# The steps of each head's softmax placed one by one, with longer planned durations for ScalarE and VectorE from attention on

## The chip, the cores and the metric

The kernel runs on one core of a Trainium2 chip. The metric is the device time of one execution in microseconds; the number quoted for the kernel before is the median of its timed runs. Engines are named as in the profile: PE is the matrix engine (PEld its weight loads), ACT is ScalarE, DVE is VectorE, POOL is GpSimd, SP is the queue that starts most DMAs.

## The reference, cut to what matters

One layer of a hybrid block over 528 tokens (16 meta tokens and 512 others) and 2048 channels. One projection gives the inputs of two branches. Branch A is attention of 8 heads with 4 key groups, in which an indexer picks 128 keys for each query; branch B is a gated linear recurrence. Each branch is gated, multiplied by its own 1024x2048 matrix, weighted by a sigmoid gate and added; the sum goes through a 2048x2048 output matrix.

```python
logits = einsum('bqgrd,bqkgd->bqgrk', qg, k_sel) * scale
logits = where(valid, logits, -inf)
p = softmax(logits, axis=-1)
o = einsum('bqgrk,bqkgd->bqgrd', p, v_sel)          # branch A, 8 heads
y_a = o * silu(z_a)
...
p = einsum('btnc,ncd->btnd', y, w_branch)           # two branches, 1024 -> 2048
merged = sum(sigmoid(gates) * p, axis=2)
return x + merged @ w_out                           # 2048 -> 2048
```

## The kernel before, in words

Everything is kept in 32 bits; a product of full accuracy is made of three matmuls, high by high, low by high and high by low. So each weight chunk of 128x1024 is split on the chip: ACT rounds it into `wh` (L387), DVE subtracts into `wl` (L388). The chunks stream through six buffers `raw`, and three buffers each for `wh` and `wl`. The chunk that a job of PE multiplies was split during the job before it, so a new `wh` can be written only when PE has left the job that used that buffer.

The program runs in stages. First the input projection in jobs of one or two column blocks (`run_pair`, products `px`, `py`, `pz`, `pw`), with the indexer and the recurrence between them. Then 32 branch jobs, 16 for branch B and 16 for branch A: each is 8 blocks of 3 matmuls of 128x512 into one PSUM bank `pg` (`mm3`, 24 matmuls), after which DVE multiplies the bank by the gate (`d_br`, tile `mg`). Last the output projection (`run_out`, `po`). Attention has no stage of its own: it is laid between the 24 matmuls of the branch B jobs.

A head h of attention is two tasks. `att_task(h)` loads its queries (and for an even head its group's keys and values, `kv`) by POOL's queue, lets PE make the logits (`plg`, four query tiles of 528, 400, 272 and 144 keys, in 15 matmuls), lets DVE add the mask and take the row maximum (L898, into `lg`), negates the maxima (L903), lets ACT take four exponentials with row sums (L906), lets DVE take the reciprocals (L908) and lets ACT scale the four tiles (L911). `pv_task(h)` then turns the probabilities by PE transposes into `ppt`, copies them by ACT into `pT`, `pS` and `pTH` (DVE makes the low parts `pTL` and that of `pS`), multiplies them with the values into `pov`, and lets DVE multiply by the gate tile `za`, which a DMA of POOL's queue brings (L959).

The order of all engines is written by a planner when the program is built. `Core` keeps a clock for each engine; `at` (L56) adds a cost to it for each instruction recorded, and the cost of ACT is 60 ns and 0.833 ns for each element of a row, that of DVE's two-operand form 65 ns and 1.042 ns. A task is a generator: it records some instructions and yields the planned time from which it may go on. `pump` (L223) is called after each block of 3 matmuls: it steps every task whose time, with 300 ns added, lies before PE's clock, and records what the task has next. Each engine then works strictly in the order recorded, waiting on semaphores. A PSUM bank that a task gets may still have to be read by ACT or DVE from its last use; PE then waits.

Of the kernel before, what the change touches and what calls it, by code (L numbers as in the profile page):

```python
# [13 lines left out]
OP = mybir.AluOpType  # L14
# [16 lines left out]
WAIT = object()  # L31
# [14 lines left out]
class Core:  # L46
# [3 lines left out]
    def __init__(self, nc):  # L50
        self.nc = nc
        self.clk = {"pe": 0.0, "act": 0.0, "dve": 0.0, "pool": 0.0}
        self.wr = {}
        self.ac = {}

    def at(self, eng, cost, outs, ins):  # L56
        t = self.clk[eng]
        for a in ins:
            w = self.wr.get(a.tensor.name)
            if w:  # L60
                t = max(t, w[0] + (SAME[eng] if w[1] == eng else LAT))
        for a in outs:
            w = self.ac.get(a.tensor.name)
            if w:
                t = max(t, w[0] + (0 if w[1] == eng else LAT))
        e = t + cost
        self.clk[eng] = e
        for a in ins:
            w = self.ac.get(a.tensor.name)
            if not w or w[0] < e:  # L70
                self.ac[a.tensor.name] = (e, eng)
        for a in outs:
            self.wr[a.tensor.name] = (e, eng)
            self.ac[a.tensor.name] = (e, eng)
        return e + LAT
# [24 lines left out]
    def act(self, out, in_, f, **kw):  # L100
        self.nc.scalar.activation(out, in_, f, **kw)  # L101
        outs = [out] + ([kw["accum_out"]] if "accum_out" in kw else [])
        ins = [in_] + [v for v in kw.values() if not isinstance(v, (int, float)) and v is not kw.get("accum_out")]
        return self.at("act", 60 + 0.833 * self.n(in_), outs, ins)

    def tt(self, out, a, b, op):
        self.nc.vector.tensor_tensor(out, a, b, op=op)  # L107
# [75 lines left out]
def hybrid_kernel(ctx, tc, x, meta, vecs, w_in, rows, w_branch, w_out,  # L183
# [7 lines left out]
    E = Core(nc)  # L191
# [23 lines left out]
    def spawn(gen, prio=1):  # L215
        t = Task(gen, prio)
        i = len(tasks)
        while i and tasks[i - 1].prio > prio:
            i -= 1
        tasks.insert(i, t)  # L220
        return t
# [41 lines left out]
    def slot(name, dt=F32):  # L263
        return S.get(name, dt)
# [529 lines left out]
    def vs_task():  # L794
        while len(stored) < 17:
            yield WAIT
        yield from room(9)
        vx3.extend((slot("vS", F32R), slot("pS", F32R), slot("pS", F32R), slot("v3")))
        vS, v3 = vx3[0], vx3[3]
        nc.gpsimd.dma_start(v3[:, :512], v3d)  # L800
        vx = slot("vx")
        nc.gpsimd.dma_start(vx[:, :64], vxd)
        for t in vx3[:3]:
            E.pool([t], [], T // 2, lambda v: v.memset(t[:96, :512].bitcast(F32), 0.0))
        yield E.clk["pe"] + 6000.0
        pm = yield from bank("pvm")
        for g in range(4):
            e = E.tr(pm[:16, 128 * g:128 * g + 128], vx[:, 16 * g:16 * g + 16], ident)
        S.put(vx)
        yield e  # L810
        E.act(vS[0:16, :512], pm[:16], AF.Copy)
        E.act(vS[32:48, :512], pm[:16], AF.Copy)
        e = E.tt(vS[64:80, :512], pm[:16], vS[0:16, :512].bitcast(F32), OP.subtract)
        B1.put(pm)
        yield e
# [36 lines left out]
    att = {}  # L852

    def att_task(h):
        g = h // 2
        while not vx3 or h and att.get(h - 1, 0) < 1 or not topk_done():
            yield WAIT
        yield from room(2 if g in kTH else 6, 6)
        qH, qL = slot("qH", F32R), slot("qL", F32R)
        for i, t in enumerate((qH, qL)):  # L860
            nc.gpsimd.dma_start(t[:, :512].bitcast(F32), qd_[h][i])
        if g not in kTH:
            for d, src, n in ((kTH, kd_[g][0], T), (kTL, kd_[g][1], T), (vH, vd_[g][0], 512), (vL, vd_[g][1], 512)):
                d[g] = slot("kv", F32R)
                nc.gpsimd.dma_start(d[g][:, :n].bitcast(F32), src)
        yield E.clk["pe"] + 10000.0
        while h and att[h - 1] < 2 or len(S.free) < 8:
            yield WAIT
        sm = small[h % 2]
        ps, pbs, vs = {}, {}, {}  # L870
        for qt in (3, 2, 1, 0):
            kq = KQ[qt]
            sl = slice(128 * qt, 128 * qt + 128)
            if kq > 512:
                pb = yield from pair("plg")
                parts = [(pb[:, c, :264], slice(264 * c, 264 * c + 264)) for c in range(2)]
                vs[qt] = pb[:, :, :264]
            else:
                if qt:
                    pb = yield from bank("plg")  # L880
                vs[qt] = pb[:, :kq] if qt else pb[:, KQ[1]:KQ[1] + kq]
                parts = [(vs[qt], slice(0, kq))]
            pbs[qt] = pb
            for o, ks in parts:
                E.mm(o, qH[:, sl], kTH[g][:, ks], True, False)
                E.mm(o, qH[:, sl], kTL[g][:, ks], False, False)
                e = E.mm(o, qL[:, sl], kTH[g][:, ks], False, True)
            if qt == 3:
                e3 = e
        S.put(qH, qL)  # L890
        att[h] = 1
        yield e3 + 600
        col = lambda qt, i: sm[:, 4 * qt + i:4 * qt + i + 1]
        for qt in (3, 2, 1, 0):
            kq = KQ[qt]
            xs = ps[qt] = slot("lg")
            f2 = (lambda a: a.rearrange("p (a b) -> p a b", a=2)) if kq > 512 else (lambda a: a)
            E.dve([xs, sm], [pbs[qt], bias[qt]], kq, lambda vv: vv.tensor_tensor_reduce(  # L898
                f2(xs[:, :kq]), vs[qt], f2(bias[qt][:, :]), SC, NEG, OP.add, OP.max, col(qt, 0)))
            if qt != 1:  # L900
                (B2 if kq > 512 else B1).put(pbs[qt])
        allc = lambda i: sm.rearrange("p (q i) -> p q i", i=4)[:, :, i]
        E.ts(allc(1), allc(0), -1.0, None, OP.mult)  # L903
        for qt in (3, 2, 1, 0):
            xs = ps[qt][:, :KQ[qt]]
            e = E.act(xs, xs, AF.Exp, bias=col(qt, 1), accum_out=col(qt, 2))  # L906
        yield e + 1200
        E.dve([sm], [sm], 4, lambda vv: vv.reciprocal(allc(3), allc(2)))  # L908
        for qt in (3, 2, 1, 0):
            xs = ps[qt][:, :KQ[qt]]  # L910
            e = E.act(xs, xs, AF.Copy, scale=col(qt, 3))  # L911
        att[h] = 2
        pv_tasks.append(spawn(pv_task(h, ps, e + 1000), 1))

    pv_tasks = []

    def pv_task(h, ps, e):
        g = h // 2
# [21 lines left out]
        pb, e = yield from turn(3)  # L940
        yield e
        for b in (3, -1, 0, 1, 2):
            n = 512 - 128 * max(b, 0)
            kp = 128 if b >= 0 else 16
            if b == 3:
                tH, tL = slot("pT"), None
                e = E.act(tH[:, :n], pb[:, :n], AF.Copy)
            elif b < 0:
                E.act(pS[0:16, :n], pb[:16, :n], AF.Copy)
                E.act(pS[64:80, :n], pb[:16, :n], AF.Copy)  # L950
                e = E.tt(pS[32:48, :n], pb[:16, :n], pS[0:16, :n].bitcast(F32), OP.subtract)
            else:
                tH, tL = slot("pTH", F32R), slot("pTL", F32R)
                E.act(tH[:, :n], pb[:, :n], AF.Copy)
                e = E.tt(tL[:, :n], pb[:, :n], tH[:, :n].bitcast(F32), OP.subtract)
            B1.put(pb)
            if b == 3:
                z = slot("za")
                nc.gpsimd.dma_start(z[:, :512], zad[h])  # L959
            if b != 2:  # L960
                pb, e2 = yield from turn(0 if b == -1 else (-1 if b == 3 else b + 1))
            yield e
            o = po[:, 512 - n:]
            if b == 3:
                E.mm(o, v3[:, gs], tH[:, :n], True, False, loose=True)
                S.put(tH)
            elif b < 0:
                E.mm(o, vS[:96, gs], pS[:96, :n], False, False, loose=True)
            else:
                wh, wl = vH[g][:, 128 * b:128 * b + 128], vL[g][:, 128 * b:128 * b + 128]  # L970
                E.mm(o, wh, tH[:, :n], False, False, loose=True)
                E.mm(o, wh, tL[:, :n], False, False, loose=True)
                e = E.mm(o, wl, tH[:, :n], False, b == 2, loose=True)
                S.put(tH, tL)
        yield e
        e = E.tt(z[:, :512], po, z[:, :512], OP.mult)
# [593 lines left out]
    jobs = [Job("in", C_KI, 80, True, done=d_kiwi)]  # L1570
# [33 lines left out]
            gate_pair()  # L1604
    while gates:
        gate_pair()
    jobs[-1].pre = lambda: (spawn(vs_task(), 1), [spawn(att_task(h), 1) for h in range(8)])
    pairs = [j for j in jobs if j.kind == "pair"]
    for n in (1, 0):
        for p in range(8):  # L1610
# [213 lines left out]
```

## Time and profile before

| | us |
|---|---|
| timed runs: median of 3 (lowest, highest) | 1529.73 (1529.63, 1530.08) |
| the profiled execution's own time | 1525.58 |
| its span, first to last instruction | 1523.8 |
| DVE busy in the span | 1173.5 (77%) |
| ACT busy in the span | 679.5 (45%) |
| POOL busy in the span | 199.4 (13%) |

The profile is of one execution, which took 4.15 us less than the median of the timed runs; the two are kept apart below. In the span attention lies at about 1130 to 1260 us. Busy time of PE is the union of its matmul records; a record lasts longer than the distance from one matmul to the next (a 128x512 record some 0.40 us, the next one starting 0.23 us later), so the first 0.17 us of a pause do not show as idle.

### The profile page before, as it was taken

The page shows a single profiled execution, that of the slowest core. Times are in us where ns is not written, and L with a number is a line of the kernel's source. Part 1 is how long each engine was busy: PE and PEld are TensorE (multiplying, and loading weights), DVE is VectorE, ACT ScalarE, POOL GpSimd, SP SyncE. Part 2 cuts the span into 40 slices and gives each one's busy share as a digit, 9 for nine tenths or more (in the row PEclk, how much of TensorE's full clock was granted, in tenths as well). Part 3 has the DMA queues.
Part 4 walks back from the last instruction along what each step waited for, and adds up shares of the span by engine and source line. Part 5 has one row for each costly group of instructions (what it writes and reads, how often), then busy time and mean ns, then how long its engine had stood idle before and what let it go on. Part 6 is the DMA issues. An engine that isn't in the chain of part 4 may idle for free.

```text
span 1523.8 us, 30986 instructions
## 1 busy us (share of the span) xinstructions
PE 1500.0 (98%) x12648; PEld 1417.8 (93%) x12648; DVE 1173.5 (77%) x1971; ACT 679.5 (45%) x1048; POOL 199.4 (13%) x241
## 2 busy tenths in 40 slices
PE   7999999999999999999999999999999999999998
PEld 6888899999999999999999999999998778889998
DVE  7799999999998778677768776786665455878675
ACT  5555454444444443443443444444455652334332
POOL 3100000001111101001000010000032210102222
PEclk9999999999999999999999999999999999999999
DMA  9223368867787756766675667567796434448773
GB/s 267 83 70 83 96 158 190 186 162 187 200 205 198 194 134 142 180 149 161 146 174 133 160 157 177 143 142 174 188 296 216 160 118 125 143 139 216 212 212 89
DMA packets 300959, 250.08 MB, mean 164 GB/s; under 512 B 12932, under 2 KB 267920, under 8 KB 300816
## 3 DMA queue, kind: packets, MB, share of 16 engines
q1 hardware_dynamic: 274080, 167.95, 37.6%
q0 software_dynamic: 20656, 72.81, 24.2%
q10 hardware_dynamic: 6080, 7.34, 1.4%
q8 instruction: 99, 1.62, 0.4%
q14 instruction: 44, 0.36, 0.1%
HBM read 168.00 MB, written 27.62 MB: 128 GB/s over the span
## 4 chain that ended last, share of the span: by engine, by line
PE 86%; issue 7%; ACT 2%; DVE 2%; POOL 1%; DMA 1%; ACTq 0%; POOLq 0%; DVEq 0%
PE pg L93 18%; PE pz L91 14%; PE py L91 14%; PE px L91 14%; PE po L91 10%; PE pw L91 7%; PE phl L93 1%; PE psc L93 1%; ACT lg L101 1%; PE pho L93 1%; PE pov L91 1%; PE phs L93 1%; DVE lg L898 1%; PE px L97 1%; DMA kv<-vd 1%
## 5 line engine op out<-in xcount | busy, mean ns | idle before, releaser
L101 ACT ACTIVATE wh<-raw 128x1024 fp32r<-128x1024 f32 x304 | 322.0, 1060 | 490.1 <-PE pz L91 130.6
L107 DVE TENSOR_TENSOR wl<-raw,wh 128x1024 fp32r<-128x1024 f32 x302 | 370.9, 1229 | 140.7 <-ACT wh L101 139.0
L91 PE MATMUL px<-hH,wh 128*128 128x256 f32 (+1 forms) x672 | 193.5, 288 | 0.0
L91 PE MATMUL px<-hH,wl 128*128 128x256 f32 (+1 forms) x672 | 189.2, 282 | 0.0
L91 PE MATMUL px<-hL,wh 128*128 128x256 f32 (+1 forms) x672 | 189.2, 281 | 0.0
L101 ACT ACTIVATE wh<-sum 128x1024 fp32r<-128x1024 f32 x100 | 106.1, 1061 | 181.5 <-PE pw L91 70.7
L91 PE MATMUL po<-wh,mh 128*128 128x256 f32 x896 | 158.5, 280 | 0.5 <-DVE xq L107 0.5
L107 DVE TENSOR_TENSOR wl<-sum,wh 128x1024 fp32r<-128x1024 f32 x100 | 127.0, 1270 | 34.4 <-ACT wh L101 34.3
L91 PEld LDWEIGHTS po<-wh,mh 128*128 128x128 f32 x896 | 137.4, 189 | 0.8 <-DVE xq L107 0.7
L91 PEld LDWEIGHTS px<-hH,wh 128*128 128x128 f32 x672 | 126.5, 188 | 0.9
L91 PEld LDWEIGHTS px<-hH,wl 128*128 128x128 f32 x672 | 126.6, 188 | 0.0
L91 PEld LDWEIGHTS px<-hL,wh 128*128 128x128 f32 x672 | 126.4, 188 | 0.0
L91 PE MATMUL po<-wl,mh 128*128 128x256 f32 x448 | 125.6, 280 | 0.0
L91 PE MATMUL py<-tT,wh 128*128 128x256 f32 (+1 forms) x672 | 124.7, 284 | 0.0
L91 PE MATMUL pw<-tT,wh 128*128 128x256 f32 (+1 forms) x672 | 124.6, 285 | 0.0
L91 PE MATMUL pz<-tT,wh 128*128 128x256 f32 (+1 forms) x672 | 123.5, 283 | 0.0
L116 POOL DMA_DIRECT2D raw<-raw x50 | 43.2, 863 | 519.9 <-DVE sum L107 510.1
L91 PEld LDWEIGHTS py<-tT,wh 128*128 128x128 f32 x672 | 103.3, 188 | 0.5
L91 PEld LDWEIGHTS pw<-tT,wh 128*128 128x128 f32 x672 | 103.2, 188 | 0.2
L91 PEld LDWEIGHTS pz<-tT,wh 128*128 128x128 f32 x672 | 103.1, 188 | 0.2
L93 PE MATMUL pg<-yH,wh 128*128 128x512 f32 x256 | 103.0, 402 | 0.1
L93 PE MATMUL pg<-yL,wh 128*128 128x512 f32 x256 | 100.8, 394 | 0.0
(317 smaller groups left out, 3792.8 us busy)
## 6 DMA issues: line engine op xcount, KB each, us to landing
raw<-in_w_in_dram SPq DMA_DIRECT2D x192, 512.0 KB, 4.6
raw<-raw POOLq DMA_DIRECT2D x50, 512.0 KB, 5.3
raw<-sum POOLq DMA_DIRECT2D x50, 512.0 KB, 6.1
raw<-in_w_branch_dram SPq DMA_DIRECT2D x32, 512.0 KB, 5.0
raw<-in_w_out_dram SPq DMA_DIRECT2D x32, 512.0 KB, 4.3
gd<-g SPq DMA_DIRECT2D x32, 256.0 KB, 5.1
g<-gd POOLq DMA_DIRECT2D x30, 256.0 KB, 3.4
x<-in_x_dram SPq DMA_DIRECT2D x16, 256.0 KB, 5.5
```

What stands on the lines that cost most here:

```text
L91: self.nc.tensor.matmul(out, lhsT, rhs, start=start, stop=stop, skip_group_check=True)
L93: self.nc.tensor.matmul(out, lhsT, rhs, start=start, stop=stop)
L97: self.nc.tensor.transpose(out, in_, ident)
L101: self.nc.scalar.activation(out, in_, f, **kw)
L107: self.nc.vector.tensor_tensor(out, a, b, op=op)
L116: self.nc.gpsimd.dma_start(out, a, accum_op=OP.add)
L898: E.dve([xs, sm], [pbs[qt], bias[qt]], kq, lambda vv: vv.tensor_tensor_reduce(f2(xs[:, :kq]), vs[qt], f2(bias[qt][:, :]), SC, NEG, OP.add, ...
```

## The change

The planner's costs: from the last pair job on, each ACT instruction is planned 130 ns longer and each DVE instruction 85 ns longer, and an ACT instruction with a row sum another 190 ns. This stays in force to the end of the program, so that branch A's jobs and the first part of the output projection are ordered by it too. The steps of a head: `att_task` now yields after the negation, after each exponential, after the reciprocal and after each scaling, where it recorded each group in one go; the fixed allowances of 600, 1200 and 1000 ns are gone. `pv_task` is spawned after the first scaling (the 528 tile) instead of the last, and waits for the other three before it loads `za` and goes on. No instruction is added or taken away on any engine; every engine but SP has another order.

```diff
@@ class Core @@
+        self.more = {"pe": 0.0, "act": 0.0, "dve": 0.0, "pool": 0.0}
...
-        e = t + cost
+        e = t + cost + self.more[eng]
...
@@ act() @@
-        return self.at("act", 60 + 0.833 * self.n(in_), outs, ins)
+        c = 190 if "accum_out" in kw and self.more["act"] else 0
+        return self.at("act", 60 + 0.833 * self.n(in_) + c, outs, ins)
@@ att_task() @@
-        yield e3 + 600
+        yield e3
...
-        E.ts(allc(1), allc(0), -1.0, None, OP.mult)
+        yield E.ts(allc(1), allc(0), -1.0, None, OP.mult)
         for qt in (3, 2, 1, 0):
             xs = ps[qt][:, :KQ[qt]]
             e = E.act(xs, xs, AF.Exp, bias=col(qt, 1), accum_out=col(qt, 2))
-        yield e + 1200
-        E.dve([sm], [sm], 4, lambda vv: vv.reciprocal(allc(3), allc(2)))
+            yield E.clk["pe"]
+        yield e
+        yield E.dve([sm], [sm], 4, lambda vv: vv.reciprocal(allc(3), allc(2)))
         for qt in (3, 2, 1, 0):
             xs = ps[qt][:, :KQ[qt]]
             e = E.act(xs, xs, AF.Copy, scale=col(qt, 3))
-        att[h] = 2
-        pv_tasks.append(spawn(pv_task(h, ps, e + 1000), 1))
-
-    pv_tasks = []
+            if qt == 3:
+                att[h] = 2
+                pv_tasks.append(spawn(pv_task(h, ps, e), 1))
+            yield E.clk["pe"]
+        scaled[h] = e
+
+    pv_tasks, scaled = [], {}
@@ pv_task() @@
             if b == 3:
+                while h not in scaled:
+                    yield WAIT
+                yield scaled[h]
                 z = slot("za")
                 nc.gpsimd.dma_start(z[:, :512], zad[h])
@@ last pair job @@
-    jobs[-1].pre = lambda: (spawn(vs_task(), 1), [spawn(att_task(h), 1) for h in range(8)])
+    jobs[-1].pre = lambda: (E.more.update(act=130.0, dve=85.0), spawn(vs_task(), 1), [spawn(att_task(h), 1) for h in range(8)])
```

On ACT, at the change from head 3 to head 4. Before: the four exponentials of head 4 (`lg_14660` to `lg_14666`), and behind them head 3's copies out of its transposes, `pTH_14683` and `pT_14696`.

```order
L101 ACTIVATE pTH_14634<-ppt_14594 128x512
L101 ACTIVATE lg_14660,small_171<-lg_14660,small_171 128x528
L101 ACTIVATE lg_14662,small_171<-lg_14662,small_171 128x400
L101 ACTIVATE lg_14664,small_171<-lg_14664,small_171 128x272
L101 ACTIVATE lg_14666,small_171<-lg_14666,small_171 128x144
L101 ACTIVATE pTH_14683<-ppt_14638 128x384
L101 ACTIVATE pT_14696<-ppt_14691 128x128
```

After the change the same place reads as follows, where head 3's tiles are `lg_14516` to `lg_14522` and head 4's are `lg_14676` to `lg_14682`.

```order
L102 ACTIVATE wh_14617<-raw_14133 128x1024
L102 ACTIVATE lg_14516<-lg_14516,small_172 128x528
L102 ACTIVATE pTH_14630<-ppt_14591 128x384
L102 ACTIVATE lg_14518<-lg_14518,small_172 128x400
L102 ACTIVATE lg_14520<-lg_14520,small_172 128x272
L102 ACTIVATE pT_14652<-ppt_14639 128x128
L102 ACTIVATE lg_14522<-lg_14522,small_172 128x144
L102 ACTIVATE pTH_14665<-ppt_14634 128x256
L102 ACTIVATE pS_13908<-ppt_14694 16x512 x2
L102 ACTIVATE lg_14676,small_171<-lg_14676,small_171 128x528
```

Head 3's copy `pT` stood behind head 4's four exponentials; it now stands between head 3's own scalings, four rows ahead of the first exponential of head 4.

On PE, the same place before: `ppt_14691` is the first transpose of head 3 (of the tile `lg_14514`), whose bank ACT copies into `pT`; `ppt_14700` needs that bank again.

```order
L97 MATMUL ppt_14687<-ident,lg_14395 128x128
L97 MATMUL ppt_14687<-ident,lg_14393 128x128
L97 MATMUL ppt_14691<-ident,lg_14514 128x128
L93 MATMUL pg_14611<-yH_14013,wh_14444 128x512
L93 MATMUL pg_14611<-yL_14014,wh_14444 128x512
L93 MATMUL pg_14611<-yH_14013,wl_14445 128x512
L97 MATMUL ppt_14700<-ident,lg_14520 16x128
L97 MATMUL ppt_14700<-ident,lg_14518 16x128
L97 MATMUL ppt_14700<-ident,lg_14516 16x128
L97 MATMUL ppt_14700<-ident,lg_14514 16x128
L91 MATMUL pov_14690<-pT_14696,v_556_13909 128x128
```

After the change, right behind the first block of three matmuls of branch B's job `pg_14616`, with head 3's first transpose `ppt_14639` of `lg_14516`:

```order
L92 MATMUL pov_14486<-pTH_14587,kv_14251 128x512
L92 MATMUL pov_14486<-pTL_14588,kv_14251 128x512
L92 MATMUL pov_14486<-pTH_14587,kv_14253 128x512
L98 MATMUL ppt_14634<-ident,lg_14383 128x128
L98 MATMUL ppt_14634<-ident,lg_14381 128x128
L98 MATMUL ppt_14639<-ident,lg_14516 128x128
L94 MATMUL pg_14616<-yH_13961,wh_14444 128x512
L94 MATMUL pg_14616<-yL_13962,wh_14444 128x512
L94 MATMUL pg_14616<-yH_13961,wl_14445 128x512
L94 MATMUL plg_14645<-kv_14529,qH_14525 128x264
```

and five rows further, where the bank that `pT` copies is wanted next, by head 4's logits `plg_14658`:

```order
L94 MATMUL plg_14645<-kv_14529,qL_14526 128x264
L94 MATMUL pg_14616<-yH_13965,wh_14444 128x512
L94 MATMUL pg_14616<-yL_13966,wh_14444 128x512
L94 MATMUL pg_14616<-yH_13965,wl_14445 128x512
L94 MATMUL plg_14658<-kv_14529,qH_14525 128x400
L94 MATMUL plg_14658<-kv_14531,qH_14525 128x400
L94 MATMUL plg_14658<-kv_14529,qL_14526 128x400
```

Three matmuls stood between the transpose that `pT` copies and the next use of its bank (`ppt_14700`), and head 3's first product with `pT` came right behind; now twelve matmuls stand there (`plg_14658`), and the product `pov_14638` follows 31 matmuls behind the transpose.

On POOL's queue, the loads for heads 1 to 4 (`za` the gate tile, `qH` and `qL` queries, `kv` keys), before:

```order
L959 DMA za_14369<-zad_156 128x512
L861 DMA qH_14409<-qd_0_144 128x512
L861 DMA qL_14410<-qd_1_145 128x512
L861 DMA qH_14527<-qd_0_146 128x512
L861 DMA qL_14528<-qd_1_147 128x512
L865 DMA kv_14531<-kd_0_126 128x528
```

and after:

```order
L863 DMA qH_14390<-qd_0_144 128x512
L863 DMA qL_14391<-qd_1_145 128x512
L968 DMA za_14394<-zad_156 128x512
L863 DMA qH_14525<-qd_0_146 128x512
L863 DMA qL_14526<-qd_1_147 128x512
L867 DMA kv_14529<-kd_0_126 128x528
```

The load of `za` for head 1 went behind the queries of head 3; the key loads that follow have the same place.

## The prediction

> **What bounds the kernel now.** First the page's head and its chain by engine.
>
> ```profile
> span 1523.8 us, 30986 instructions
> PE 1500.0 (98%) x12648; PEld 1417.8 (93%) x12648; DVE 1173.5 (77%) x1971; ACT 679.5 (45%) x1048; POOL 199.4 (13%) x241
> PE 86%; issue 7%; ACT 2%; DVE 2%; POOL 1%; DMA 1%; ACTq 0%; POOLq 0%; DVEq 0%
> ```
>
> PE bounds it: it is idle for only 1523.8 − 1500.0 = 23.8 us in all, and the change takes no work from it. So the most that a new order can win is idle time of PE in the part that it reorders. The windows by stage say where that is (length of the window, then busy us of PE, PEld, DVE, ACT and POOL, granted clock, DMA share, GB/s): attention, the rest of the branch jobs, most of the output projection, and two stretches of 10 us in attention.
>
> ```profile
> 1130.00:1260.00 130.00, 121.26 (x652) 101.29 (x651) 71.36 (x160) 76.88 (x173) 24.07 (x46) 1.00 0.56 177
> 1260.00:1355.00 95.00, 95.00 (x414) 77.05 (x413) 64.08 (x98) 30.23 (x42) 8.52 (x16) 1.00 0.43 133
> 1355.00:1500.00 145.00, 145.00 (x1209) 143.82 (x1208) 105.78 (x107) 58.45 (x62) 35.44 (x27) 1.00 0.76 200
> 1220.00:1230.00 10.00, 8.30 (x42) 6.39 (x40) 6.12 (x16) 5.11 (x13) 2.65 (x5) 1.00 0.55 185
> 1230.00:1240.00 10.00, 8.26 (x53) 7.42 (x54) 4.83 (x14) 5.13 (x14) 0.00 (x0) 1.00 0.18 52
> ```
>
> From 1260 to 1500 us PE never pauses: nothing can be won there, only lost. In attention it pauses for 130.00 − 121.26 = 8.74 us, while ACT is busy for 59% and DVE for 55%. Neither is short of time there; they do the right work in the wrong order. The waits of PE from 1100 to 1250 us, complete (what waits, on what, us in total, times, longest):
>
> ```profile
> PE ppt L97 <- ACT pT L101: 5.3, 2, 3.2
> PE plg L93 <- DVE pS L107: 1.4, 1, 1.4
> PE ppt L97 <- DVE pTL L107: 1.4, 2, 1.1
> PE pov L91 <- ACT pT L101: 0.5, 1, 0.5
> ```
>
> Six waits, 8.6 us, all for copies that return a bank of transposes. The timeline of the second longest (start, duration, engine, what; the idle time before and its releaser in brackets):
>
> ```profile
> 1194.09 0.74 ACT L101 ACTIVATE lg<-lg,small 128x528 f32<-128x528 f32 x1 [3.62 <-DVE small L121]
> ...
> 1195.94 0.40 ACT L101 ACTIVATE lg<-lg,small 128x144 f32<-128x144 f32 x1
> ...
> 1196.34 0.47 ACT L101 ACTIVATE pTH<-ppt 128x384 fp32r<-128x384 f32 x1
> 1196.71 0.26 ACT L101 ACTIVATE pT<-ppt 128x128 f32<-128x128 f32 x1
> 1194.54 0.40 PE L93 MATMUL pg<-yH,wl 128*128 128x512 f32 x1
> 1197.02 0.60 PE L97 MATMUL ppt<-ident,lg 128*16 128x128 f32 x4 [2.08 <-ACT pT L101]
> ```
>
> ACT, idle for 3.62 us before, goes through head 4's four exponentials (1194.09 to 1196.34), and only then makes head 3's `pTH` and `pT`. PE needs the bank of `pT`. The longest wait has the same form, with head 6's four scalings ahead of head 5's copies:
>
> ```profile
> 1228.18 0.38 PE L97 MATMUL ppt<-ident,lg 128*128 128x128 f32 x2
> 1229.18 1.97 ACT L101 ACTIVATE lg<-lg,small 128x528 f32<-128x528 f32 x4 [1.81 <-DVE small L908]
> 1231.06 0.47 ACT L101 ACTIVATE pTH<-ppt 128x384 fp32r<-128x384 f32 x1
> 1231.43 0.26 ACT L101 ACTIVATE pT<-ppt 128x128 f32<-128x128 f32 x1
> 1231.74 0.61 PE L97 MATMUL ppt<-ident,lg 128*16 128x128 f32 x4 [3.17 <-ACT pT L101]
> ```
>
> A stall costs more than its idle entry. For the price of a matmul:
>
> ```profile
> 1172.38 4.18 PE pg L93 x18
> ```
>
> 4.18/18 = 0.232 us from one 128x512 matmul to the next, while a record lasts 0.40, so the first 0.17 us of every stall lies under a record: 0.17 × 6 = 1.0. What the stalls take is **8.74 + 1.0 = 9.7 us**.
>
> **The change, part by part.** *The costs of ACT and DVE.* The old planner put a 528-column exponential at 60 + 0.833 × 528 = 500 ns, without its row sum. By form, 1130 to 1260 us (busy us, mean ns):
>
> ```profile
> L101 ACT ACTIVATE wh<-raw 128x1024 fp32r<-128x1024 f32 x14 | 14.7, 1049 | 0.5 <-PE pg L93 0.4
> L101 ACT ACTIVATE lg<-lg,small 128x528 f32<-128x528 f32 x16 | 11.8, 737 | 42.5 <-DVE small L121 29.5 <-DVE small L908 12.9
> L101 ACT ACTIVATE pS<-ppt 16x512 fp32r<-16x512 f32 x16 | 9.3, 583 | 4.8 <-PE ppt L97 4.7
> L101 ACT ACT_TABLE_LOAD x1 | 1.3, 1283 | 0.0
> L898 DVE CUSTOM_DVE_ANT_0 lg<-plg,bias 128x528 f32<-128x528 f32 x8 | 5.6, 702 | 3.0 <-PE plg L93 3.0
> L898 DVE CUSTOM_DVE_ANT_0 lg<-plg,bias 128x400 f32<-128x400 f32 x8 | 4.6, 569 | 0.0
> ```
>
> It measures 737 (exponentials and scalings together). The group of four in the timeline took 2.25 us and was planned as 4 × 60 + 0.833 × 1344 = 1.36; with 130 + 190 ns more for each it is planned as 2.64. The planner therefore lets PE do more work before it counts on what comes behind. *The steps.* One exponential or scaling is now recorded at a time, so a copy can stand between two, and waits for one operation (at most 0.74 us) instead of 2.25. The orders above show it: head 3's `pT` leaves its place behind head 4's exponentials, twelve PE matmuls instead of three precede the next use of its bank, and the first product with `pT` stands 31 matmuls behind the transpose. The same holds for `pTL` and DVE's `pS`, which wait behind the same groups. Followed through all eight heads in the new order, with durations from the trace, each of the six waits is covered. Removed: **−9.7**.
>
> *The earlier spawn of `pv_task`.* A head's first transposes now follow its first scaling, and two places become late. (1) Head 3: ahead of `ppt_14639` PE does six matmuls of its job (6 × 0.232) and two transposes of about 0.1 (0.38 for two records, less 0.17, halved), 1.6 us, while ACT does `wh` and a scaling, at most 1.05 + 0.74 = 1.8: 0.2 lost. (2) Head 5: `ppt_14977` takes the bank that DVE's 400-column score step frees. Behind `plg_14944` DVE needs 0.70 + 0.57 = 1.27. PE does nine matmuls meanwhile, 2448 of the logits' 4032 columns:
>
> ```profile
> 1147.04 1.92 PE plg L93 x15
> ```
>
> 1.92 × 2448/4032 = 1.17, so 0.1 is lost, 0.25 with a handover. For what a walk by means misses I add some 0.35: **+0.8** in all, with bounds of 0 and 4.5 (the partial rival).
>
> *The load of `za`* waits for the last scaling, so POOL issues it later and the key loads behind it in its queue may wait too. The price of such a load (the longest in the chain, and the group's median at the end of its row):
>
> ```profile
> 1122.17 8.05 DMA kv<-vd
> kv<-vd POOLq DMA_DIRECT2D x8, 256.0 KB, 6.6
> ```
>
> In the new order some 12 us of PE work stand between the key load's place and `plg_14944`, which needs it: 4 us are left over the 8.05, and I take 0. If that cover goes, it costs the slower rival's price.
>
> *Branch A and the output projection* keep the raised costs. DVE's gate products are recorded later there, and PE could then wait for a bank; but DVE is busy for 64.08 of 95 us and 105.78 of 145, so it keeps up: 0, up to one product (about 0.7 us) at a place. *SP* keeps its order, and no instruction is added.
>
> [...] The row shows one table load of 1283 ns in the stage, although 32 exponentials already alternate with copies by heads; in the order, both programs have three in all. [...]
>
> *The clock.* In the rows of 1220 to 1240 us, with the stall of 3.17, the granted clock is 1.00. [...]
>
> Sum against the profiled execution's own time: 1525.58 − 9.7 + 0.8 = 1516.7, 8.9 less. The median of the runs is 4.15 above that execution, and I carry the difference over: 1529.73 − 8.9 = **1520.8**.
>
> **The rivals.** *Partial: ACT falls behind at job boundaries.* The planner does not model that a `wh` buffer is free only when PE leaves its job:
>
> ```profile
> 1157.94 1.06 ACT L101 ACTIVATE wh<-raw 128x1024 fp32r<-128x1024 f32 x1 [0.20 <-PE pg L93]
> 1157.98 0.39 PE L93 MATMUL pg<-yH,wh 128*128 128x512 f32 x1
> ```
>
> `wh` starts as the next job does, and holds ACT for 1.05 us. If a softmax step stands in front and the copy behind, the copy is up to 1.05 + 0.74 late, where the planner counted nothing. For: the finer steps put more of these at boundaries. Against: 8 to 12 matmuls (1.9 to 2.8 us) usually separate transpose and next use. At 13 boundaries (between the 14 `wh` rows) and about a third of a `wh`, 0.35 us, each: 4.5 come back, 1529.73 − 9.7 + 4.5 + 0.8 = 1525.3.
>
> *The change does not do what it says.* The planned clock may stay off by more than the new numbers mend; each stall then only moves to another pair of copy and scaling. For: the added figures are constants, while forms differ (16x512 `pS`, 583 ns, runs longer than its 486 planned by 97, not 130). Against: the order itself shows the copies moved ahead. 1529.7, give or take 3.
>
> *Slower: POOL's queue.* POOL works in order. If a `za` load waits for ACT's late scalings, the queries and keys behind it are issued late. It decides from a delay of 12 − 8.05 = 4 us on. A head lasts about 16 us (130/8), so waiting for a later step of the next head can reach 10; three groups' key loads, each 6 us late, give +18: 1520.8 + 18 = 1539. For: the loads are long, and 0.56 of DMA time is taken. Against: in the order `za` passed only queries, and the key loads kept their place.
>
> **How the numbers follow.** Forecast 55% (1519.7 to 1523.2: savings of 10 to 6.5). Partial 23% (1523.2 to 1526.7). Nothing 14% (1526.7 to 1532.7, most within 0.2%, 3.1 us, about what a measurement can tell from no change). Slower 8%. Faster by over 0.2% is below 1526.7: 0.55 + 0.23 = 0.78; same 0.14; slower 0.08. The range goes from 1518 (1529.73 − 9.7 = 1520.0 with every stall gone and nothing lost, less 2 for pauses shorter than 0.17 us, which lie wholly under records) to 1527.5, the end of the partial case and the edge of the next; about 0.2 is left out.
>
> **What would show it.** Right: PE busy for nearly all of attention, the waits for `pT` and `pTL` gone or under 0.5 us in total each, `pTH` and `pT` standing between exponentials in ACT's timeline, and 1260 to 1500 us still without a pause. Partial: a wait of 0.3 to 0.5 us a few matmuls behind many job starts, with `wh` before its releaser. Slower: `plg` waiting for `kv`, with POOL's `za` issue waiting for ACT. [...]

## The result, and the profile after

| | before | after |
|---|---|---|
| timed runs: median (lowest, highest), 6 each, us | 1529.82 (1529.63, 1531.07) | 1516.65 (1515.74, 1517.89) |
| the profiled execution's own time, us | 1525.58 | 1516.59 |
| its span, us | 1523.8 | 1514.8 |
| PE busy in the span, us | 1500.0 (98%) | 1498.3 (99%) |

The ratio of the runs is 0.9913, with a 95% interval of 0.9901 to 0.9926: 13.2 us faster, well clear of no change. Of all runs in this document one (of `e_late`, 2430.63 us at a granted clock of 0.557) was in a slow state and is left out of every number. The prediction was 1520.8 with a range of 1518.0 to 1527.5: the sign was right, and the gain was larger than the range allowed. The two profiled executions differ by only 9.0 us. That gap of 4 us between the timed runs and the profiles is the question of this study.

First the windows by stage of the kernel after (columns as for before):

```profile
1130.00:1260.00 130.00, 129.81 (x699) 110.05 (x698) 79.79 (x168) 81.95 (x179) 25.98 (x49) 1.00 0.60 188
1260.00:1355.00 95.00, 95.00 (x424) 77.67 (x423) 65.12 (x101) 29.13 (x41) 8.33 (x15) 1.00 0.45 128
1355.00:1500.00 145.00, 145.00 (x1234) 145.00 (x1233) 106.67 (x104) 60.61 (x64) 38.69 (x29) 1.00 0.74 199
```

In attention PE is idle for 0.19 us where it was idle for 8.74. Behind it PE still never pauses. All waits of PE from 1100 to 1250 us are now one line:

```profile
PE ppt L98 <- DVE small L900: 0.2, 1, 0.2
```

The place of the stall of 2.08 us now reads as follows in the timelines of ACT and PE:

```profile
1187.62 0.51 ACT L102 ACTIVATE lg<-lg,small 128x272 f32<-128x272 f32 x1
1188.04 0.26 ACT L102 ACTIVATE pT<-ppt 128x128 f32<-128x128 f32 x1
1188.19 0.41 ACT L102 ACTIVATE lg<-lg,small 128x144 f32<-128x144 f32 x1
1188.50 0.37 ACT L102 ACTIVATE pTH<-ppt 128x256 fp32r<-128x256 f32 x1
...
1188.93 0.39 PE L94 MATMUL pg<-yH,wl 128*128 128x512 f32 x1
1189.16 0.53 PE L94 MATMUL plg<-kv,qH 128*128 128x400 f32 x2
```

Head 3's `pT` stands between two of the head's own scalings and is done at 1188.30; the next matmul on its bank (`plg`, 1189.16) starts without a wait.

One thing makes the profiles look closer than they are. PE's first instruction waits for the first load:

```profile
PE pc L98 <- DMA vrow<-in_vecs_dram: 8.2, 1, 8.2
```

In the profile of before the same line has 7.0 us. Counted from PE's first instruction, before took 1523.8 − 6.96 = 1516.8 and after 1514.8 − 8.21 = 1506.6: 10.2 us less. So 3 us are left that no row of the first two profiles shows.

### The profile page after: what moved, and what is told of

It is laid out like the page before. It is cut to its first block, busy times and chain, and to the rows that moved or that the text cites. A ratio compares the mean times of both kernels' runs of the same rounds, so it can differ in the third digit from the quotient of the medians.

```text
span 1514.8 us, 30989 instructions
## 1 busy us (share of the span) xinstructions
PE 1498.3 (99%) x12648; PEld 1418.5 (94%) x12648; DVE 1176.8 (78%) x1971; ACT 679.3 (45%) x1048; POOL 199.8 (13%) x241
## 4 chain that ended last, share of the span: by engine, by line
PE 97%; ACT 1%; issue 1%; DVE 0%; DMA 0%; POOL 0%; ACTq 0%; DVEq 0%; POOLq 0%
PE pg L94 21%; PE pz L92 16%; PE py L92 16%; PE px L92 16%; PE po L92 10%; PE pw L92 8%; PE phl L94 2%; PE psc L94 1%; PE pov L92 1%; PE plg L94 1%; PE pho L94 1%; PE ppt L98 1%; PE phs L94 1%; PE px L98 1%; PE pqa L98 0%
```

## The experiments

Twelve runs were made, two of them of the kernel before, unchanged. Where a line gives a time or a ratio to "before", it is of the kernel before run beside it on the same chip.

**Before again, and its clock.** `b1` and `b2` are the kernel before, unchanged.

> The kernel before, unchanged, with a new profile. Open is why the timed runs differ by 13.2 us and the two profiled executions by 9.0. Theory one (the first profile of before was a lucky execution and something in its timed runs costs about 4 us more): this profile takes about 1529.7 us, the same six stalls of PE in attention come back at 9.7 us or more, and the trace shows where the other 4 us lie (a longer stall, a lower granted clock, a later start). Theory two (the offset of 4 us belongs to the profiled execution of before as such): this profile again takes about 1525.6 while its timed runs lie at 1529.7.

> The kernel before once more, for a third profile. Clock theory: if this execution takes 1529 us or more, the trace shows a granted clock below 1 in some window, most likely behind the stall of 3.4 us in attention. Rival: 1529 us with a granted clock of 1.00 throughout and a longer stall or a later start.

`b1`: 1529.27 us (1527.48 to 1531.34, 11 runs); its profiled execution took 1527.48, the lowest of all, with a granted clock of 1.00 and the six stalls in their places (PE's list again has 5.3 for `pT` and 1.4 for `pS`). That lies between the 1529.7 of theory one and the 1525.6 of theory two, so `b1` alone does not decide. `b2` is one execution, of 1529.33 us, and its mean granted clock is 0.997. The windows of its trace:

```profile
1196.00:1198.00 2.00, 0.39 (x3) 0.29 (x4) 0.56 (x1) 1.56 (x8) 0.00 (x0) 0.93 0.00 0
1198.00:1200.00 2.00, 2.00 (x11) 1.92 (x10) 0.19 (x1) 1.17 (x2) 0.00 (x0) 0.50 0.04 12
1200.00:1202.00 2.00, 2.00 (x9) 1.74 (x7) 0.68 (x2) 1.20 (x3) 0.00 (x0) 0.72 0.00 0
1202.00:1230.00 28.00, 27.02 (x143) 22.11 (x141) 16.90 (x38) 15.49 (x37) 7.41 (x14) 1.00 0.57 188
1230.00:1232.00 2.00, 0.00 (x0) 0.00 (x0) 0.04 (x1) 1.87 (x4) 0.00 (x0) 0.96 0.31 78
1232.00:1234.00 2.00, 1.31 (x7) 1.08 (x8) 0.56 (x1) 0.89 (x4) 0.00 (x0) 0.50 0.63 184
1234.00:1236.00 2.00, 2.00 (x9) 2.00 (x8) 1.01 (x2) 1.79 (x4) 0.00 (x0) 0.50 0.00 0
1236.00:1238.00 2.00, 2.00 (x8) 1.71 (x8) 0.69 (x2) 0.00 (x0) 0.00 (x0) 0.50 0.00 0
1238.00:1240.00 2.00, 2.00 (x14) 1.93 (x14) 0.40 (x1) 0.00 (x0) 0.00 (x0) 0.83 0.00 0
```

The third number from the end is the granted clock. Behind each of the two longest stalls

```profile
1197.61 0.95 PE L97 MATMUL ppt<-ident,lg 128*16 128x128 f32 x4 [2.11 <-ACT pT L101]
1232.69 1.02 PE L97 MATMUL ppt<-ident,lg 128*16 128x128 f32 x4 [3.17 <-ACT pT L101]
```

it falls to a half: in windows of 0.2 us, from 1197.6 to 1201.2 (3.4 us of half clock) and from 1231.8 to 1238.8 (6.8 us). There one 128x512 matmul starts 0.43 us behind the other, elsewhere 0.23. PE works for 9.4 of those 10.2 us, and at half clock loses half of that, some 4.7 us; some of it comes back, because PE, being slower, finds later copies ready (the waits for `pTL` fall from 1.4 to 0.5 us). By the starts of ACT's `wh` instructions, `b2` was 0.7 us ahead of `b1` before attention and 2.4 behind it at 1285 us: 3.1 us lost there. (At 1500 us it is 1.9 behind, because `b1` itself loses 0.5 between 1390 and 1412; why stays open.)

In these experiments 65 executions of the kernel before list a clock; 4 of them have 1.00, with a median of 1527.0 us; 61 have 0.994 to 0.999. The median rises as the clock falls: 1528.9 at 0.999 (11 runs), 1529.4 at 0.998 (28 runs), 1531.1 at 0.997 (16 runs). Of the changed kernel's runs all 6 have 1.00. So **the kernel before loses about 2.5 us to the clock in its median run, and something in nearly all of them, and its first profile was one of the few without that**. With its 1525.58 us that profile is also 1.5 below the median of the four at 1.00, so not all of the gap is the clock. That was theory one of `b1`, with the place as `b2`'s clock theory had it.

**Which pauses lower the clock.** In the changed kernel PE never pauses in branch A, so pauses of a chosen length can be put there. `st8`, `st4` and `st2` add 28 copies in 8, 4 and 2 pauses, `st8k2` and `st8k1` two and one copies in each of 8 pauses:

```diff
+        if job.kind == "br" and job.n == 0:
+            nst[0] += 1
+            for i in range(4 if nst[0] in STALL else 0):
+                E.tr(b[:, 128 * i:128 * i + 128], ident, ident)
+            for i in range(STALL.get(nst[0], 0)):
+                E.act(b[:, :], b[:, :], AF.Copy)
         for ch in job.chunks:
```

`STALL` holds the jobs and the copies of each, for `st4` `{1: 7, 3: 7, 5: 7, 7: 7}`.

> The changed kernel with eight pauses of PE added in branch A's jobs, where it otherwise never pauses: in each, PE writes a bank, ACT copies it in place 3 or 4 times (28 copies in all) and PE waits for that. The pauses should be about 1.6 to 2.2 us each, some 15 us in all. If a pause costs what its length is, the time is 1516.5 plus the pauses as the trace has them, and the granted clock of the runs stays 1.0. If pauses of any length lower the clock, it is 3 us or more above that sum.

> The same 28 copies in four pauses of 7, about 3.5 to 4 us each, near the longest stall of the kernel before (3.4). Clock theory (a pause as long as that stall makes the clock drop in most executions, and that is the part of the 13.2 us which the first profile of before does not show): granted clock 0.996 to 0.999 in most runs, and up to 1.7 us for each pause, 2 to 7 us in all, above 1516.5 plus the pauses of the trace. Rival (a long pause costs only its length, and the runs of before are slower for another reason): granted clock 1.0 and the time of the sum.

> The same 28 copies in two pauses of 14, about 7 us each. Clock theory: both pauses are followed by a stretch at a lower granted clock in nearly every execution, the trace shows it, and the time is 2 to 4 us above 1516.5 plus the pauses. Rival: 1516.5 plus the pauses.

> The eight added pauses of PE in branch A with 2 copies each, so about 1.3 us idle each (the traces of the runs with 3, 4 and 7 copies had 1.90, 2.51 and 4.35: 0.61 a copy), 10.3 us in all. With the transposes (8 x 0.4) and the part of a pause that lies under a record (8 x 0.17) that is 1516.5 + 15 = 1531. Theory (only pauses of about 2 us or more make a window of 3.41 us run at half clock): clock 1.0 and 1530 to 1532. Rival (a pause of any length near 1 us does): 5 to 7 windows, 1.7 us each, 1540 to 1543 and a clock of 0.992 or 0.993.

> The same eight pauses with one copy, about 0.7 us idle each, 5.4 us in all; with transposes and covered part 1516.5 + 10 = 1526.5. Theory: clock 1.0 and 1525.5 to 1527.5. Rival: windows at half clock here too, 1530 or more.

PE's wait for these copies in each trace (total, times, longest), in the order `st8k1`, `st8k2`, `st8`, `st4`, `st2`:

```profile
PE pg L94 <- ACT pg L102: 5.4, 8, 0.7
```

```profile
PE pg L94 <- ACT pg L102: 10.3, 8, 1.3
```

```profile
PE pg L94 <- ACT pg L102: 17.6, 8, 2.5
```

```profile
PE pg L94 <- ACT pg L102: 17.4, 4, 4.4
```

```profile
PE pg L94 <- ACT pg L102: 17.3, 2, 8.6
```

| run | pauses, us idle each | time, us | clock of the runs | without clock effect | excess | half clock in branch A, by the trace |
|---|---|---|---|---|---|---|
| `st8k1` | 8 x 0.67 | 1528.02 | 1.00 (8 of 10 runs) | 1527.9 | 0.1 | none |
| `st8k2` | 8 x 1.28 | 1532.55 | 1.00 (7 of 10 runs) | 1532.8 | −0.2 | none |
| `st8` | 4 x 1.90, 4 x 2.51 | 1550.75 | 0.992 to 0.993 | 1540.1 | 10.7 | 7 stretches of 3.4 us |
| `st4` | 4 x 4.35 | 1544.03 | 0.993 to 0.994 | 1537.0 | 7.0 | 3.4, 3.4, 6.8, 3.4 us |
| `st2` | 2 x 8.64 | 1540.56 | 0.991 to 0.993 | 1535.4 | 5.2 | 6.8 and 10.2 us, 9.7 of the 17 within the pauses |

The sum without a clock effect is 1516.65, the idle time of the pauses and 0.73 us for each pause: `st8k1` is (1528.02 − 1516.65)/8 = 1.42 us a pause for 0.67 idle, `st8k2` 1.99 for 1.28, so 0.75 and 0.71 come on top (four transposes, and the part under a record). These two runs set that price, so their own excess is near 0 by construction; the clock of their runs and traces is what speaks for them. The others test the price, on another chip, which may be worth 1 us (the kernel before has a median of 1530.51 us on the chip of the first two and of 1529.60 on theirs). Two windows of `st8`, behind a pause of 1.90 us that ends at 1295.53:

```profile
1294.00:1296.00 2.00, 0.47 (x2) 0.42 (x3) 0.65 (x1) 1.94 (x4) 1.06 (x2) 1.00 0.00 0
1296.00:1298.00 2.00, 2.00 (x7) 1.56 (x6) 1.53 (x3) 0.74 (x2) 0.01 (x1) 0.52 0.80 262
```

The clock is 1.00 over the 2 us in which the pause ends, and 0.52 over the next 2. Seven of the eight pauses of 1.90 or 2.51 us (all but the first) were followed by 3.4 us at half clock, 7 x 1.7 = 11.9 us by the trace against 10.7 in the time. The seven stretches start some 10.2 us apart, so they are not seven independent trials; but all four runs have a clock of 0.992 or 0.993. Pauses of 1.28 us cost no clock in the trace, and in 7 of 10 runs none (the other three have 0.998 or 0.999). In the expectations this was the rival of `st8` and the theory of `st8k2` and `st8k1`, whose times lie 0.5 us above the ranges given; the clock theory of `st4` held but for its size, whose bound of 7 us the excess just reaches. In `st2` the excess is above its 4 us; PE works through 3.1 and 4.3 us of the two stretches, worth 3.7 us, and the trace also has 3.4 us of half clock at 18 to 22 us, in the start. The profiles of `e_costs` and `e_group` have such a stretch in the start too; what brings it there was not tried.

**Where a pause falls.** A limit on the length of a pause does not explain all traces: before and `b1` have pauses of 2.08 and 3.17 us, and `e_steps` (below) one of 2.97, with no fall of the clock behind them. What PE did in the last 3.4 us does not tell them apart either. These are windows of that length, with PE's busy time behind it: of before, the one up to the end of its stall of 3.17 us and the one behind it; and one each of `b2` (the same stall), `st8` and `e_group` (below), up to a fall of the clock.

```profile
1228.33:1231.74 3.41, 0.23 (x4) 0.00 (x1) 0.94 (x3) 2.50 (x6) 0.00 (x0) 1.00 0.44 126
1231.74:1235.15 3.41, 3.41 (x24) 3.21 (x25) 1.90 (x4) 2.05 (x4) 0.00 (x0) 1.00 0.09 28
```

```profile
1228.44:1231.86 3.42, 1.08 (x6) 0.66 (x5) 1.59 (x3) 1.73 (x4) 0.00 (x0) 1.00 0.15 38
```

```profile
1292.66:1296.08 3.42, 1.52 (x9) 1.09 (x8) 1.38 (x2) 2.35 (x4) 1.06 (x2) 1.00 0.00 0
```

```profile
1284.18:1287.60 3.42, 1.68 (x7) 0.91 (x7) 1.81 (x3) 0.72 (x2) 0.00 (x0) 1.00 0.01 2
```

In before PE was busy for 0.23 us there and the clock stayed at 1.00; in `b2`, `st8` and `e_group` it was busy for 1.08, 1.52 and 1.68 us, and half clock followed. In the start of `e_group` the clock fell at 17.9 us, with PE busy for 3.1 us from 14 to 18. So the same stall lowered the clock in one execution of the kernel before and not in two others, and what decides it was not shown.

**Costs alone, steps alone.** `e_costs` is the kernel before with `E.more` and the 190 ns; `e_steps` is the changed kernel without them:

```diff
-    jobs[-1].pre = lambda: (E.more.update(act=130.0, dve=85.0), spawn(vs_task(), 1), [spawn(att_task(h), 1) for h in range(8)])
+    jobs[-1].pre = lambda: (spawn(vs_task(), 1), [spawn(att_task(h), 1) for h in range(8)])
```

> Only the planner's raised costs, without the softmax steps placed one by one, the early spawn and the wait ahead of za. If the costs do most of it, the time is within 2 us of the changed kernel (1516.6 to 1518.6) and the waits for pT are gone. If the one-by-one steps are needed, because a group of four on ACT (2.25 us) still stands in front of a copy, some of the six stalls stay or others appear: 3 to 6 us above the changed kernel, 1520 to 1523.

> Only the steps placed one by one, with the early spawn and the wait ahead of za, at the old costs. If the steps do most of it: 1516 to 1519. If the old costs (500 ns for an exponential that takes 737) make the planner place copies too late for PE whatever the size of a step, and the early spawn pulls transposes ahead of scalings that are not done, the stalls stay or grow: 1524 to 1532.

`e_costs`: 1528.36 us (1526.17 to 1529.53; before 1529.34; ratio 0.9989, 0.9980 to 0.9999). `e_steps`: 1521.41 us (1520.48 to 1522.39; ratio 0.9944, 0.9930 to 0.9957). All four readings missed: the costs alone are worth 1 us, and the steps alone 7.9, between the two ranges given for them. In attention `e_costs` still waits 1.8 us for a `pT` and 1.5 for a `pS`. Its waits from 1255 to 1345 us:

```profile
PE pg L94 <- ACT yH L102: 2.1, 2, 1.4
PE pov L92 <- DVE pS L109: 1.3, 1, 1.3
PE ppt L98 <- ACT lg L102: 0.6, 1, 0.6
PE pg L94 <- DVE yL L109: 0.4, 2, 0.2
```

Its last head ends late. The last `yH` of attention starts at

```profile
1284.58 0.63 ACT L102 ACTIVATE yH<-za 128x512 fp32r<-128x512 f32 x1 [1.78 <-DVE za L109]
```

and at 1255.88 in the changed kernel, 1262.12 before; branch A's first jobs need it. In `e_steps` one long stall remains (2.97 us; three others sum to 1.1). PE and ACT there:

```profile
1140.18 1.28 ACT L102 ACT_TABLE_LOAD   x1
1141.93 0.73 ACT L102 ACTIVATE lg<-lg,small 128x528 f32<-128x528 f32 x1 [0.47 <-DVE small L123]
...
1144.52 1.26 ACT L102 ACTIVATE lg<-lg,small 128x528 f32<-128x528 f32 x2 [0.25 <-DVE small L911]
...
1145.31 0.33 PE L98 MATMUL ppt<-ident,lg 128*128 128x128 f32 x1 [2.97 <-ACT lg L102]
```

Head 0's first transpose is recorded behind its first scaling, at a moment that the low costs put too early: ACT has the table load and four exponentials still ahead. The granted clock of `e_steps` is 0.997 or 0.998 in three of its four runs, so part of its loss may be the clock; four runs are too few to tell (the one at 1.00 took 1522.18).

**Groups without the allowances.** `e_group` is `e_costs` without the fixed 600, 1200 and 1000 ns:

```diff
-        yield e3 + 600
+        yield e3
...
-        yield e + 1200
+        yield e
...
-        pv_tasks.append(spawn(pv_task(h, ps, e + 1000), 1))
+        pv_tasks.append(spawn(pv_task(h, ps, e), 1))
```

> The raised costs in the kernel before with the fixed allowances of 600, 1200 and 1000 ns taken away, the four exponentials and the four scalings still recorded in one go, the spawn still behind the last scaling. If the run with the costs alone gained so little because its allowances, added to costs that are now right, made each head late (its last head ended so late that PE waited in branch A's first jobs), this is near the changed kernel, 1516 to 1520. If the groups of four are to blame, stalls behind a group stay: 1522 to 1528.

1532.88 us (1530.68 to 1533.84; before 1530.51; ratio 1.0013, 1.0004 to 1.0023): slower than before, outside both readings, though the one that blames the groups is the nearer. So the allowances are not the reason for the small gain. PE again waits for the late `yH` of the last heads in branch A's first jobs, and the clock falls behind it:

```profile
1274.43 0.80 PE L94 MATMUL pg<-yH,wh 128*128 128x512 f32 x1 [2.77 <-ACT yH L102]
...
1286.73 0.50 PE L94 MATMUL pg<-yH,wh 128*128 128x512 f32 x1 [1.44 <-ACT yH L102]
```

```profile
1274.00:1284.00 10.00, 8.86 (x28) 6.55 (x29) 2.71 (x5) 5.00 (x11) 0.00 (x0) 0.50 0.00 0
1284.00:1287.00 3.00, 1.48 (x7) 0.94 (x5) 1.41 (x3) 0.90 (x2) 0.00 (x0) 0.97 0.00 0
1287.00:1291.00 4.00, 3.78 (x10) 2.78 (x10) 2.72 (x5) 2.12 (x2) 0.00 (x0) 0.57 0.01 2
```

So raised costs with large groups make the heads late: their last `yH` starts at 1286.05 us in `e_group`, 1284.58 in `e_costs`. Why the planner delays groups so much was not tried; `pump` records nothing once ACT's planned clock is 3 us ahead of PE's, and four exponentials at the raised costs fill 2.64 of that; whether this is the reason is not shown.

**The early spawn, za, and the costs behind attention.** `e_late` undoes the early spawn:

```diff
-            if qt == 3:
-                att[h] = 2
-                pv_tasks.append(spawn(pv_task(h, ps, e), 1))
-            yield E.clk["pe"]
+            if qt:
+                yield E.clk["pe"]
         scaled[h] = e
+        att[h] = 2
+        pv_tasks.append(spawn(pv_task(h, ps, e), 1))
```

`e_undo` loads `za` ahead of the wait, and ends the raised costs with head 7:

```diff
+                z = slot("za")
+                nc.gpsimd.dma_start(z[:, :512], zad[h])
                 while h not in scaled:
                     yield WAIT
                 yield scaled[h]
-                z = slot("za")
-                nc.gpsimd.dma_start(z[:, :512], zad[h])
...
         if h == 7:
             S.put(*vx3)
+            E.more.update(act=0.0, dve=0.0)
```

> The changed kernel with only the early spawn undone: the product task of a head is spawned behind its last scaling, and the next head's score steps go on from there too. If the spawn behind the first scaling is needed to bring the last head home in time for branch A: 1518 to 1522 with pauses of PE behind 1255 us. If it is worth nothing: 1515.7 to 1517.7.

> The changed kernel with two parts undone that the prediction put at 0: za's load is issued ahead of the wait for the scalings, and the raised costs end with head 7, so that branch A and the output projection are ordered by the old costs. If both are worth nothing: within 1 us of the changed kernel (1515.7 to 1517.7). If the raised costs win something behind 1260 us, 1 to 4 us above it; if the late load of za holds up the key loads in POOL's queue, below it.

`e_late`: 1516.17 us (three runs, 1515.96 to 1516.68; ratio 0.9906, 0.9886 to 0.9926). `e_undo`: 1516.14 us (1515.75 to 1516.64; ratio 0.9909, 0.9896 to 0.9923). Both lie within 0.6 us of the changed kernel, as the reading "worth nothing" had it. (`e_undo` takes back two parts at once, so two effects of opposite sign could hide each other.) Their PE rows in attention say the same, `e_late` first:

```profile
1130.00:1255.00 125.00, 125.00 (x675) 106.14 (x674) 73.73 (x160) 78.62 (x173) 25.44 (x48) 1.00 0.61 195
```

```profile
1130.00:1250.00 120.00, 119.82 (x653) 101.68 (x652) 73.70 (x160) 78.28 (x173) 24.96 (x47) 1.00 0.62 197
```

No version was clearly faster than the changed kernel, and in attention PE has next to nothing left to win.

## Why the prediction was right in its sign and wrong in its size

**Right: the stalls and what covers them.** "What the stalls take is 9.7 us": all six are gone. By the distance from one matmul's start to the next, PE's pauses from 1125 to 1262 us sum to 12.9 us before and 3.4 after (those of over 0.08 us): 9.5 less. Taking each form's median distance as the ordinary one gives 13.1 and 3.2, 9.9 less. The signs named for the forecast are all there: `pTH` and `pT` between ACT's softmax steps, no `pT` or `pTL` in PE's waits, no pause behind 1260 us.

**Too high: the 0.8 us given back.** The late place of head 5 is real, as a wait of 0.19 us, and 0.36 beyond the ordinary distance of two starts (0.1 was said, or 0.25 with 0.15 for a handover, an estimate of the author's), and for the step that was named: DVE's 400-column score step ends at 1217.56, 0.15 us ahead of the transpose.

```profile
1216.99 0.57 DVE L900 CUSTOM_DVE_ANT_0 lg<-plg,bias 128x400 f32<-128x400 f32 x1
...
1217.25 0.27 PE L94 MATMUL plg<-kv,qL 128*128 128x144 f32 x1
1217.71 0.30 PE L98 MATMUL ppt<-ident,lg 128*128 128x128 f32 x1 [0.19 <-DVE small L900]
```

Head 3's 0.2 and the 0.35 added for what a walk misses did not come. That is about 0.5 us of the sum.

**Wrong: no part for the clock.** The prediction has the granted clock of 1.00 in the rows with the stall of 3.17 us, and its sum nothing for the clock. This is the step that failed. It took the granted clock of one execution for that of the timed runs, and with it the next step failed, that the median is 4.15 us above that execution "and I carry the difference over". Most of the difference was the clock, which the change removes together with the stalls: with 2.5 us more the sum would have been 1518.3, within the range. The median of the runs of before is about 2.5 us above those at a clock of 1.00, and `b2` shows the place. The timed runs alone say the same: from the 1527.0 of the four executions of before at 1.00 it is 10.4 us to the changed kernel's 1516.65, where 8.9 was forecast, and the other 2.8 of the 13.2 lie between 1527.0 and before's median of 1529.82. The profiles, counted from PE's first instruction, give 10.2. So of the 4.3 us that the forecast fell short, some 2.5 to 2.8 are the clock and 0.5 the give-back above. The rest, about 1 us, is open; it is within the spread of single executions (`b1`, also at 1.00, is 1.2 us longer than the first profile of before, counted from PE's first instruction, and the four at 1.00 reach from 1526.17 to 1528.42).

That the stalls bring the lower clock is shown from both sides. The three kernels without a long pause in attention, the changed one, `e_late` and `e_undo`, have 1.00 in all 13 runs, and pauses put back into the changed kernel (`st8`, `st4`, `st2`) lower the clock again. How long a pause has to be for that was not shown: in `st8` pauses of 1.90 us were enough, and in before those of 2.08 and 3.17 us were not.

**The rivals.** *Partial:* no wait for `pT` or `pS` behind a job's start is left; the boundaries cost nothing. *Nothing:* did not happen to the change as a whole, but it is what `e_costs` shows, where some stalls moved within attention and others to branch A's first jobs. *Slower by POOL's queue:* PE's list has no wait for `kv`, and `e_undo` has the time of the changed kernel; the cover was enough. *Table loads:* attention has one, of 1.28 us, after the change as before.

**Which part does it.** The prediction gave the costs and the steps one common sum. Apart they are worth 1.0 and 7.9 us, and together 13.2. Each of these times holds the clock's part as well: 9 of 10 runs of `e_costs` and 3 of 4 of `e_steps` are below 1.00. The steps cure most; that it is because a copy can stand between two of them is read from ACT's timeline at head 3. The costs with the steps also cure the transposes that were recorded too early (the 2.97 us of `e_steps`). The costs with the old groups make heads late. The early spawn, the wait ahead of `za` and the costs behind attention were put at 0 or near it, and are worth nothing that was measured.

## What to carry to other kernels

Before a median is compared with a profile, look at the granted clock of every run: here, where the profiled execution has 1.00 and most of the timed runs 0.997 to 0.999, the pauses of the matrix engine cost the median run some 2.5 us more than their length, and curing them won that too. In an order written by a planner, the size of a step matters as much as its cost: a copy that another engine waits for should stand behind one operation and not behind a group of four, and a longer planned cost on too large a step won almost nothing here, or lost 2 us (`e_group`). A part of a change that wins little alone may still be needed with the other.

## What the runs showed of the hardware

At a granted clock of a half, one 128x512 matmul started 0.43 us behind the other (`b2`), elsewhere 0.23. In attention and branch A half clock came in stretches of 3.4 us or two or three times that: 3.4 and 6.8 us in `b2`, seven of 3.4 in `st8`, 3.4 and 6.8 in `st4`, 6.8 and 10.2 in `st2`. It followed pauses of 4.35 us in all four cases (`st4`), those of 1.90 and 2.51 us in 7 of 8 (`st8`), and those of 1.28 us in none of 8 (`st8k2`). A stall of 3.17 us left the clock at 1.00 in before and `b1` and not in `b2`, one of 2.97 us left it at 1.00 in `e_steps`; so the length alone does not decide, and what does was not shown. For the same 28 copies, few long pauses lost less to the clock than many short ones: two pauses 5 us, four 7 and eight 11; with eight pauses of two copies or one each, the traces have no half clock in branch A.
